# Attention scores as 256-column products of split queries and keys, and powers of lambda put in place by ScalarE

## The chip, the cores and the metric

The kernel runs on one core of one Trainium2 chip. TensorE (PE) multiplies, VectorE (DVE) and ScalarE (ACT) work element by element, GpSimd (POOL) does little here, and SyncE (SP) issues the DMAs. The metric is device time in microseconds. A change of about 0.2% is the least that a measurement of this kernel can tell from none.

## What is computed

One hybrid decoder layer over 256 tokens of 1024 features: an input projection, 32 diagonal complex state-space groups beside eight causal attention heads of 64, an output projection, a layer norm, a mixture of 16384 single-neuron experts, and a second layer norm. With one block of 256 keys the attention is plain causal attention. What matters here:

```python
lam_bar = jnp.exp(lam * dt)
b_bar = ((lam_bar - 1.0) / lam)[:, :, None] * b_c
...
s_own = jnp.einsum('bhqd,bhkd->bhqk', qf, ko) * scale
s_own = jnp.where(k_pos[None, :] <= q_pos[:, None], s_own, NEG)
p = jax.nn.softmax(jnp.concatenate([s_sel, s_own], axis=-1), axis=-1)
```

The state-space part needs the products of B and C with the powers lam_bar, lam_bar squared and so on (four time steps are taken together).

## The kernel before

The kernel is written with a scheduler that orders the instructions of each engine by the order of tracing and by what is free, and places all waits. A pool's tile with a tag has a fixed number of buffers (`bufs`); a new tile waits until the last user of the buffer's old tile is done. Instructions of one engine run in the order shown by the scheduler; an engine that waits holds up everything behind it.

The stages in order: the mixer (input projections, state space, attention, output projection, first norm), the queries and their top-16 lists on VectorE, the first matrices of the experts (`u_wide`, line 911), the gates, the second matrices (`v_mm`, line 1175) and the last norm. From the queries on the work is large fp32r products, with weights cut into a high and a low part: `split` (line 67) casts the high part on ScalarE (line 71) and subtracts on VectorE (line 72). The mixer's pieces are traced in the order of the words in `CFG['order']` (line 46), each word a branch of `do` (line 665).

Pieces that the change and the prediction touch:

- **Input projection.** `tokproj` (line 170, word u) and `chproj(1, ...)` (line 179, word q) multiply in plain fp32: one product is two passes in the trace. `chproj(2, ...)` (word k) multiplies split keys' weights with split tokens (`xsplit`, line 196: mixh and mixl), in fp32r: 96 products of 256 columns, in four quarters of 24. Both calls of `chproj` take four PSUM banks from the pool tag "w" (`pbank`, line 102, four buffers), and ScalarE copies each bank to `qk` (line 191), which is fp32.
- **State space.** `powers` (line 408) makes B or C times powers of lambda: two products per part on VectorE (lines 421 and 422), and then, since pairs of groups go to different columns of the block-diagonal Bbd or Cbd, two 64-partition operations (line 426) that add or subtract and put the result in place. `s5_min` (line 447, word min) turns Bbd on TensorE in eight groups of four transposes (line 452), and ScalarE copies each to MinT (line 454). `s5_rot` (line 466) builds rotations on VectorE in `big` buffers that `powers` uses too.
- **Masks.** `masks` (line 593, word mask, first in the order) makes `mb`, 128x128 in bf16, and `identb`.
- **Scores.** `attend(b)` (line 611) takes one block b of 128 queries, two heads at a time. A head's operands lie on 64 partitions. For each block of keys it makes a 128x128 product in fp32 (line 623) and adds the mask to the diagonal one by a product of identb and mb (line 627), on 128 partitions. For b = 0 only the first 128 keys count; for b = 1 all 256. Then VectorE takes the maximum, ScalarE the exponentials, TensorE transposes them (line 637) and ScalarE copies them to pTs. Between the heads stand the value projection's products (line 217).
- **Shared buffers.** x0 (tag "x2") holds the transposed tokens xT in its first half and the second block's transposed probabilities in the other; later x2, the normalised tokens, takes its place, and last the final weights (line 1210).

Of the kernel before, what the change touches and what calls it, by code (L numbers as in the profile page):

```python
# [8 lines left out]
F32 = mybir.dt.float32  # L9
# [32 lines left out]
def f32(ap):  # L42
    return ap.bitcast(F32)


CFG = dict(order='mask zero u par b q min rt rot xs ks k c0 c vs e0 e1 s0 v v a0 v a0 v a0 a0 v s1 a1 v a1 v a1 a1 v kin p0 o0 p1 o1 glu',
# [7 lines left out]
def layer(ctx, tc, I, out, tap=None, upto=None):  # L54
# [58 lines left out]
    with ExitStack() as px:  # L113
# [6 lines left out]
        with ExitStack() as mx:  # L120
# [9 lines left out]
            x0 = const.tile([128, 2, ND * T], F32, tag="x2", name="x0")  # L130
            xT = x0[:, 0].rearrange("p (d t) -> p d t", t=T)
# [36 lines left out]
            qk = sb.tile([128, 2, 4, T], F32, name="qk")  # L168
# [10 lines left out]
            def chproj(blk, scale, parts):  # L179
# [10 lines left out]
                for m in range(4):  # L190
                    S.activation(qk[:, blk - 1, m], pt[m], AF.Copy, scale=scale)
                return mm
# [16 lines left out]
            def vproj(pt):  # L209
                for q in range(4):  # L210
                    hi, lo = M["wv", q]
                    for k in range(2):
# [6 lines left out]
                        yield  # L219

# [187 lines left out]
            def powers(L, n, xr, xi, dst, k0, sg, EE, tmp):  # L408
# [9 lines left out]
                for i, (a, b) in enumerate(((xr, xi), (xi, xr))):  # L418
# [171 lines left out]
            mb = sb.tile([128, 128], BF, name="mb")  # L590
            identb = sb.tile([128, 128], BF, name="identb")

            def masks():
# [5 lines left out]
                for j in range(4):  # L599
                    P.iota(pq[32 * j:32 * j + 32], pattern=[[0, 1]], base=j, channel_multiplier=4,  # L600
                           allow_small_or_imprecise_dtypes=True)
                V.tensor_scalar(mb, kp.rearrange("p j c -> p (j c)"), pq, NEGBIG,
                                op0=OP.is_gt, op1=OP.mult)
                V.tensor_copy(identb, ident)
# [4 lines left out]
                   x0[:, 1].rearrange("p (n i t) -> p n i t", n=4, i=2)]  # L609

            def attend(b):
# [3 lines left out]
                for n in range(4):  # L615
# [3 lines left out]
                    pt = pbank([128, 2, T])  # L619
                    for i, h in enumerate(heads):  # L620
# [740 lines left out]
```

## Time and profile before

| what | value |
|---|---|
| median of three runs | 951.42 us (950.58 to 951.55) |
| the profiled execution's own time | 949.16 us |
| its span, first to last instruction | 947.4 us |
| mean granted TensorE clock | 0.995 of full speed |
| TensorE busy | 934.4 us (99%) |
| VectorE busy | 721.7 us (76%) |
| ScalarE busy | 562.8 us (59%) |

A profile is one execution. The busy time of an engine counts instructions from start to end; products on TensorE are pipelined and their ends are modelled, so it is the distance of their starts that tells their price. A releaser (written `<-`) is what ended an engine's idle time.

### The profile page before, as it was taken

The page shows a single profiled execution, that of the slowest core. Times are in us where ns is not written, and L with a number is a line of the kernel's source. Part 1 is how long each engine was busy: PE and PEld are TensorE (multiplying, and loading weights), DVE is VectorE, ACT ScalarE, POOL GpSimd, SP SyncE. Part 2 cuts the span into 40 slices and gives each one's busy share as a digit, 9 for nine tenths or more (in the row PEclk, how much of TensorE's full clock was granted, in tenths as well). Part 3 has the DMA queues.
Part 4 walks back from the last instruction along what each step waited for, and adds up shares of the span by engine and source line. Part 5 has one row for each costly group of instructions (what it writes and reads, how often), then busy time and mean ns, then how long its engine had stood idle before and what let it go on. Part 6 is the DMA issues. An engine that isn't in the chain of part 4 may idle for free.

```text
span 947.4 us, 15305 instructions
## 1 busy us (share of the span) xinstructions
PE 934.4 (99%) x5588; PEld 810.0 (86%) x5588; DVE 721.7 (76%) x1495; ACT 562.8 (59%) x1067; POOL 11.2 (1%) x19
## 2 busy tenths in 40 slices
PE   9999999999999999999999999999999999999996
PEld 4887889998888888999999999888888888888885
DVE  9998687998988967888898996655555555555566
ACT  4526644566575667998888776554455465445550
POOL 3000010000000000000000000000000000000000
PEclk9999999999999999999999999999999999999998
DMA  7331573356555555354444445655555585555551
GB/s 290 111 113 58 173 237 112 135 179 202 195 180 198 182 195 178 134 182 156 156 157 156 157 157 178 198 189 192 198 192 190 196 285 188 193 200 189 191 198 45
DMA packets 50075, 166.18 MB, mean 175 GB/s; under 512 B 5328, under 2 KB 9936, under 8 KB 49872
## 3 DMA queue, kind: packets, MB, share of 16 engines
q1 hardware_dynamic: 50000, 165.20, 51.3%
q8 instruction: 44, 0.72, 0.3%
q14 instruction: 31, 0.25, 0.1%
HBM read 163.09 MB, written 2.10 MB: 174 GB/s over the span
## 4 chain that ended last, share of the span: by engine, by line
PE 91%; DVE 8%; issue 1%; ACT 0%; DVEq 0%; ACTq 0%
PE pg L1180 36%; PE pw L916 16%; PE pw L1264 10%; PE pw L918 10%; PE pg L1141 3%; PE pa L1264 3%; PE pw L919 2%; PE pw L768 2%; PE psb L217 1%; PE pa L871 1%; PE pw L623 1%; PE pw L498 1%; PE psb L552 1%; PE pw L648 1%; PE pw L945 0%
## 5 line engine op out<-in xcount | busy, mean ns | idle before, releaser
L72 DVE TENSOR_TENSOR lo<-raw,hi 128x1024 fp32r<-128x1024 f32 x168 | 205.6, 1224 | 151.8 <-ACT hi L71 151.6
L71 ACT CAST hi<-raw 128x1024 fp32r<-128x1024 f32 x168 | 176.9, 1054 | 171.8 <-PE pg L1180 156.5
L1180 PE MATMUL pg<-hi,wv 128*128 128x512 f32 x988 | 264.5, 389 | 0.0
L1180 PEld LDWEIGHTS pg<-hi,wv 128*128 128x128 f32 x988 | 185.4, 188 | 38.7 <-DVE wv L1111 0.2
L916 PE MATMUL pw<-x,hi 128*128 128x512 f32 x672 | 171.2, 393 | 0.0
L1180 PE MATMUL pg<-lo,wv 128*128 128x512 f32 x494 | 152.3, 389 | 0.0
L916 PEld LDWEIGHTS pw<-x,hi 128*128 128x128 f32 x672 | 124.3, 189 | 23.2
L79 DVE TENSOR_TENSOR lo<-raw,hi 128x1024 fp32r<-128x1024 f32 x96 | 117.1, 1219 | 16.8 <-ACT hi L78 15.8
L918 PEld LDWEIGHTS pw<-x,lo 128*128 128x128 f32 x768 | 104.8, 190 | 7.4
L1180 PEld LDWEIGHTS pg<-lo,wv 128*128 128x128 f32 x494 | 92.7, 188 | 19.2
L918 PE MATMUL pw<-x,lo 128*128 128x256 f32 x768 | 107.3, 282 | 0.0
L78 ACT CAST hi<-raw 128x1024 fp32r<-128x1024 f32 x96 | 101.2, 1054 | 4.2 <-PE pa L1264 2.7
L921 ACT COPY ul<-pw 128x256 f32<-128x256 f32 x96 | 35.6, 371 | 90.1 <-PE pw L919 90.1
L1135 ACT ACTIVATE o<-eq,gL 128x128 f16<-128x128 f16 x256 | 84.3, 439 | 6.0 <-DVE eq L1131 5.4
L1264 PEld LDWEIGHTS pw<-x,hi 128*128 128x128 f32 x512 | 65.9, 189 | 1.3
L1264 PE MATMUL pw<-x,hi 128*128 128x256 f32 x512 | 66.6, 283 | 0.0
L1110 ACT CAST wv<-act 128x256 fp32r<-128x256 f32 x125 | 52.3, 419 | 0.8 <-DVE act L1147 0.8
L1111 DVE TENSOR_TENSOR wv<-act,wv 128x256 fp32r<-128x256 f32 x125 | 52.0, 417 | 0.0
L1264 PE MATMUL pw<-x,lo 128*128 128x256 f32 x256 | 38.8, 292 | 0.0
L919 PE MATMUL pw<-x,hi 128*128 128x512 f32 x96 | 38.0, 396 | 0.0
L1141 PE MATMUL pg<-o,o 128*128 128x128 f16 x512 | 36.5, 219 | 0.0
L922 DVE TENSOR_TENSOR us<-pw,ul 128x256 f32<-128x256 f32 x64 | 26.8, 418 | 11.7 <-ACT ul L921 10.9
(341 smaller groups left out, 1121.0 us busy)
## 6 DMA issues: line engine op xcount, KB each, us to landing
raw<-in_u SPq DMA_DIRECT2D x128, 512.0 KB, 3.5
raw<-in_v SPq DMA_DIRECT2D x128, 512.0 KB, 3.4
raw<-in_w_q SPq DMA_DIRECT2D x12, 512.0 KB, 4.1
raw<-in_w_in SPq DMA_DIRECT2D x8, 512.0 KB, 6.2
raw<-in_w_out SPq DMA_DIRECT2D x8, 512.0 KB, 4.1
w<-in_w_in SPq DMA_DIRECT2D x7, 512.0 KB, 8.5
raw<-in_w_q SPq DMA_DIRECT2D x8, 256.0 KB, 4.9
raw<-in_w_glu SPq DMA_DIRECT2D x2, 512.0 KB, 3.4
```

The source lines that it names most:

```text
L71: S.copy(hi, raw)
L72: eng.tensor_tensor(lo, raw, f32(hi), op=OP.subtract)
L78: S.copy(hi, raw)
L79: return hi, lo, V.tensor_tensor(lo, raw, f32(hi), op=OP.subtract)
L916: PE.matmul(pt, hi[:, 128 * d:128 * d + 128], x2[:, d], start=d == 0, stop=False)
L918: PE.matmul(pt[:, 0], lo[:, 128 * d:128 * d + 128], xh[:, d], start=False, stop=False)
L919: PE.matmul(pt, hi[:, D - 128:], x2[:, ND - 1], start=False, stop=True)
L1110: S.copy(wh, of_tile(half, i))
L1135: S.activation(o2[:, 1, i // 2, :, i % 2], eq[:, i // 2, :, i % 2], AF.Copy, scale=gL[:, t0 + i:t0 + i + 1])
L1141: PE.matmul(pt[:, i], o1[:, i // 2, :, i % 2], o2[:, k, i // 2, :, i % 2], start=k == 0, stop=k == 1)
L1180: PE.matmul(acc[b][:, c], x[:, tk], w[:, 512 * c:512 * c + 512], start=first and j == 0, stop=last and j == 2)
L1264: PE.matmul(pt, w[:, 128 * d:128 * d + 128], x[:, d], start=n == 0 and d == 0, stop=n == 2 and d == ND - 1)
```

## The change

Five edits:

1. `chproj` makes a second tile, qkl: VectorE subtracts the rounded `qk`, which is fp32r now, from the scaled bank. qkl takes the buffer of xT (tag "xA").
2. `attend` makes each head's scores as three fp32r products of 256 columns on 64 partitions (high times high, low times high, high times low), and adds the mask by a fourth on 128 partitions, for both blocks of queries alike. `mb` is now a strip of 512 columns in fp32r: zeros, the triangle, zeros, the identity. A window of 256 of its columns is the mask of a block.
3. `powers` adds or subtracts on all 128 partitions at once, in place of the first product, and ScalarE copies the two halves into Bbd or Cbd.
4. The word mask moves from the front to behind c; three of the strip's four parts are written by ScalarE.
5. x0, x2 and the final weights are each two tiles (tags "xA" and "xB") in place of one.

```diff
-CFG = dict(order='mask zero u par b q min rt rot xs ks k c0 c vs e0 ...
+CFG = dict(order='zero u par b q min rt rot xs ks k c0 c mask vs e0 ...
...
-            x0 = const.tile([128, 2, ND * T], F32, tag="x2", name="x0")
-            xT = x0[:, 0].rearrange("p (d t) -> p d t", t=T)
+            xT = const.tile([128, ND, T], F32, tag="xA", name="xT")
...
-            qk = sb.tile([128, 2, 4, T], F32, name="qk")
+            qk = sb.tile([128, 2, 4, T], F32R, name="qk")
...
                 for m in range(4):
                     S.activation(qk[:, blk - 1, m], pt[m], AF.Copy, scale=scale)
+                    V.scalar_tensor_tensor(M["qkl"][:, blk - 1, m], pt[m], scale, f32(qk[:, blk - 1, m]),
+                                           op0=OP.mult, op1=OP.subtract)
...
                     E.tensor_tensor(q, b, li, op=OP.mult)
+                    E.tensor_tensor(p, p, q, op=OP.add if i and sg > 0 else OP.subtract)
                     for g in range(2):
                         sl = slice(64 * g, 64 * g + 64)
-                        o = dst[sl, i, :, k0:k0 + n, 16 * g:16 * g + 16]
-                        E.tensor_tensor(o, p[sl], q[sl],
-                                        op=OP.add if i and sg > 0 else OP.subtract)
+                        S.copy(dst[sl, i, :, k0:k0 + n, 16 * g:16 * g + 16], p[sl])
...
-                V.tensor_scalar(mb, kp.rearrange("p j c -> p (j c)"), pq, NEGBIG,
+
+                M["mb"] = mb = sb.tile([128, 4, 128], F32R, tag="Bc", bufs=1, name="mb")
+                for n in (0, 2):
+                    S.activation(mb[:, n], ident, AF.Copy, scale=0.0)
+                S.copy(mb[:, 3], ident)
+                V.tensor_scalar(mb[:, 1], kp.rearrange("p j c -> p (j c)"), pq, NEGBIG,
                                 op0=OP.is_gt, op1=OP.mult)
-                V.tensor_copy(identb, ident)
...
-                        for kb in range(nk):
-                            o = pt[:, i, 128 * kb:128 * kb + 128]
-                            PE.matmul(o, qk[r, 0, h // 2, 128 * b:128 * b + 128],
-                                      qk[r, 1, h // 2, 128 * kb:128 * kb + 128],
-                                      start=True, stop=kb != b)
-                            if kb == b:
-                                PE.matmul(o, identb, mb, start=False, stop=True)
+                        qh, ql = (x[r, 0, h // 2, 128 * b:128 * b + 128] for x in (qk, M["qkl"]))
+                        kh, kl = (x[r, 1, h // 2] for x in (qk, M["qkl"]))
+                        for j, (x, y) in enumerate(((qh, kh), (ql, kh), (qh, kl),
+                                                    (mb[:, 384:], mb[:, 128 - 128 * b:384 - 128 * b]))):
+                            PE.matmul(pt[:, i], x, y, start=j == 0, stop=j == 3)
...
+                    M["qkl"] = const.tile([128, 2, 4, T], F32R, tag="xA", name="qkl")
                     M["q"] = chproj(1, 0.125, lambda q: [(w_in(1, q), xT)])
...
-            x2 = const.tile([128, ND, 2, T], F32R, tag="x2", name="x2")
-            xh, xl = x2[:, :, 0], x2[:, :, 1]
+            xd = [const.tile([128, 4, 2, T], F32R, tag=t, name="x2") for t in ("xA", "xB")]
+            x2 = [xd[d // 4][:, d % 4] for d in range(ND)]
+            xh, xl = ([x[:, i] for x in x2] for i in range(2))
```

How it moves instructions, at three places. Line numbers of the changed kernel are one to five higher.

First, TensorE where the key projection begins, before: pw is a bank of the pool "w", psb a bank of the transposes of Bbd, and mixh and mixl are the split tokens. A wait names the engine, not the instruction.

```order
L452 MATMUL psb<-ident,Bbd 128x128 [waits DVE_49,Activation_49]
L452 MATMUL psb<-ident,Bbd 128x128 x7
L188 MATMUL pw<-mixh,hi 128x256 [waits Activation_49,Pool_49]
L188 MATMUL pw<-mixl,hi 128x256
L452 MATMUL psb<-ident,Bbd 128x128 [waits Activation_49]
L452 MATMUL psb<-ident,Bbd 128x128 x3
L452 MATMUL psb<-ident,Bbd 128x128 [waits Activation_49]
L452 MATMUL psb<-ident,Bbd 128x128 x3
L188 MATMUL pw<-mixh,lo 128x256 [waits DVE_49]
```

And with the change:

```order
L454 MATMUL psb<-ident,Bbd 128x128 [waits DVE_49,Activation_49]
L454 MATMUL psb<-ident,Bbd 128x128 x7
L454 MATMUL psb<-ident,Bbd 128x128 [waits Activation_49]
L454 MATMUL psb<-ident,Bbd 128x128 x3
L187 MATMUL pw<-mixh,hi 128x256 [waits DVE_49,Pool_49]
L454 MATMUL psb<-ident,Bbd 128x128 [waits Activation_49]
L454 MATMUL psb<-ident,Bbd 128x128 x3
L187 MATMUL pw<-mixl,hi 128x256
L454 MATMUL psb<-ident,Bbd 128x128 [waits Activation_49]
L454 MATMUL psb<-ident,Bbd 128x128 x3
```

The first key product waited for ScalarE and stood behind two groups of transposes; now it stands behind three and waits for VectorE, and five groups stand behind it.

Second, VectorE around the first four qkl instructions, with the change (rot, big: rotations; cp: the products for Cbd):

```order
L480 TENSOR_TENSOR big_131<-rot 128x64
L476 TENSOR_TENSOR big_128<-rot 128x128 [waits DVE_49]
L481 TENSOR_TENSOR rot<-big_130,big_131 128x16x4 [waits DVE_49]
L425 TENSOR_TENSOR cp<-prm,Lam 128x1024
L191 SCALAR_TENSOR_TENSOR qkl<-pw,qk 128x256 [waits PE_49,Activation_49]
L191 SCALAR_TENSOR_TENSOR qkl<-pw,qk 128x256 [waits Activation_49] x3
L477 TENSOR_TENSOR big_129<-rot 128x128 [waits DVE_49]
```

The four that free the query's banks stand behind both products for Cbd (the first some way above) and most of the rotations up to 128 columns.

Third, TensorE where the scores of the first block begin, before (mb and identb are the mask and the identity):

```order
L516 MATMUL pa<-U,MinT 128x64 x16
L623 MATMUL pw<-qk 128x128 [waits Activation_49]
L627 LDWEIGHTS identb
L627 MATMUL pw<-mb,identb 128x128
L623 MATMUL pw<-qk 128x128 [waits Activation_49]
```

And with the change, where one head is four products:

```order
L518 MATMUL pa<-U,MinT 128x64 x16
L630 MATMUL pw<-qk 128x256 [waits DVE_49]
L630 MATMUL pw<-qk,qkl 128x256
L630 MATMUL pw<-qkl,qk 128x256
L630 MATMUL pw<-mb 128x256
L630 MATMUL pw<-qk 128x256 [waits Activation_49]
```

The products of a head are longer and one mask still ends it. The first head's products now wait for VectorE too.

## Rows read from the trace of the kernel before

**Rows 1.** The page: busy time of the engines, then the last chain by engine.

```profile
PE 934.4 (99%) x5588; PEld 810.0 (86%) x5588; DVE 721.7 (76%) x1495; ACT 562.8 (59%) x1067; POOL 11.2 (1%) x19
...
PE 91%; DVE 8%; issue 1%; ACT 0%; DVEq 0%; ACTq 0%
```

**Rows 2.** Table of stretches: length, busy per engine (PE, PEld, DVE, ACT, POOL), clock, DMA.

```profile
30.00:40.00 10.00, 10.00 (x71) 8.84 (x70) 9.97 (x32) 5.83 (x12) 0.00 (x0) 1.00 0.49 142
60.00:70.00 10.00, 10.00 (x39) 7.66 (x39) 10.00 (x18) 3.51 (x10) 0.00 (x0) 0.83 0.27 89
```

**Rows 3.** Timeline, TensorE, key projection: start us, duration us, engine, line, instruction, count, idle before.

```profile
33.92 0.36 PE L188 MATMUL pw<-mixh,hi 128*128 128x256 f32 x1
...
34.40 1.14 PE L452 MATMUL psb<-ident,Bbd 128*128 128x128 f32 x8
...
42.24 0.28 PE L188 MATMUL pw<-mixh,lo 128*128 128x256 f32 x1
42.36 0.28 PE L188 MATMUL pw<-mixh,hi 128*128 128x256 f32 x1
...
46.08 0.28 PE L188 MATMUL pw<-mixl,hi 128*128 128x256 f32 x1
46.81 0.39 PE L188 MATMUL pw<-mixh,lo 128*128 128x256 f32 x1 [0.45 <-DVE lo L72]
```

**Rows 4.** Timeline, VectorE, 10 to 46 us: powers, rotations and key weights.

```profile
10.26 0.28 DVE L602 TENSOR_SCALAR mb<-kp,pq 128x128 bf16<-128x128 f32 x1
...
24.65 0.96 DVE L421 TENSOR_TENSOR big<-Bc,LamB 128x768 f32<-128x768 f32 x1
25.52 1.91 DVE L426 TENSOR_TENSOR Bbd<-big,big 64x768 f32<-64x768 f32 x2
...
37.12 0.28 DVE L475 TENSOR_TENSOR big<-rot 128x128 f32<-128x128 f32 x1
...
38.47 0.19 DVE L414 TENSOR_SCALAR nl<-Lam 128x64 f32<-128x64 f32 x1
38.57 1.22 DVE L421 TENSOR_TENSOR cp<-prm,Lam 128x1024 f32<-128x1024 f32 x1
39.71 0.42 DVE L475 TENSOR_TENSOR big<-rot 128x256 f32<-128x256 f32 x1
...
45.53 1.22 DVE L72 TENSOR_TENSOR lo<-raw,hi 128x1024 fp32r<-128x1024 f32 x1
```

**Rows 5.** Timeline, ScalarE: the cast that waits for the key projection's first quarter.

```profile
40.28 1.05 ACT L71 CAST hi<-raw 128x1024 fp32r<-128x1024 f32 x1 [1.45 <-PE pw L188]
```

**Rows 6.** Timeline, TensorE: scores of the first block (56.73 on) and the second (69.83 on).

```profile
56.73 0.49 PE L623 MATMUL pw<-qk 64*128 64x128 f32 x2
57.15 0.23 PE L627 MATMUL pw<-mb,identb 128*128 128x128 bf16 x1
57.31 0.48 PE L623 MATMUL pw<-qk 64*128 64x128 f32 x2
...
61.54 0.78 PE L217 MATMUL psb<-hi,mixh 128*128 128x512 f32 x1
...
69.83 0.71 PE L623 MATMUL pw<-qk 64*128 64x128 f32 x4
70.47 0.23 PE L627 MATMUL pw<-mb,identb 128*128 128x128 bf16 x1
70.63 0.71 PE L623 MATMUL pw<-qk 64*128 64x128 f32 x4
71.27 0.23 PE L627 MATMUL pw<-mb,identb 128*128 128x128 bf16 x1
71.31 0.48 PE L217 MATMUL psb<-wv,mixh 128*128 128x512 f32 x1
```

**Rows 7.** Timeline, TensorE's weight loads: the mask's identity and a head's keys or queries.

```profile
57.15 0.10 PEld L627 LDWEIGHTS <-identb 128*128 128x128 bf16 x1
57.31 0.18 PEld L623 LDWEIGHTS pw<-qk 64*128 64x128 f32 x1
```

More of the change, by code (lines that the diff above doesn't have):

```diff
@@ L43, in f32 @@
     return ap.bitcast(F32)
-CFG = dict(order='mask zero u par b q min rt rot xs ks k c0 c vs e0 e1 s0 v v a0 v a0 v a0 a0 v s1 a1 v a1 v a1 a1 v kin p0 o0 p1 o1 glu',
+CFG = dict(order='zero u par b q min rt rot xs ks k c0 c mask vs e0 e1 s0 v v a0 v a0 v a0 a0 v s1 a1 v a1 v a1 a1 v kin p0 o0 p1 o1 glu',
            glu='VV',
@@ L219, in vproj @@
                         yield
+            M = {}
             pw = sb.tile([128, 44, NPAIR], F32, name="pw")
@@ L601, in masks @@
                            allow_small_or_imprecise_dtypes=True)
-                V.tensor_scalar(mb, kp.rearrange("p j c -> p (j c)"), pq, NEGBIG,
+                M["mb"] = mb = sb.tile([128, 4, 128], F32R, tag="Bc", bufs=1, name="mb")
[3 more added lines that the diff above has]
+                V.tensor_scalar(mb[:, 1], kp.rearrange("p j c -> p (j c)"), pq, NEGBIG,
                                 op0=OP.is_gt, op1=OP.mult)
-                V.tensor_copy(identb, ident)
             rs = sb.tile([128, 2, 8], F32, name="rs")
             pTs = [sb.tile([128, 4, 2, 128], F32, name="pT0"),
-                   x0[:, 1].rearrange("p (n i t) -> p n i t", n=4, i=2)]
+                   const.tile([128, 4, 2, 128 * 2], F32, tag="xB", name="pT1")]
             def attend(b):
@@ L619, in attend @@
                     pt = pbank([128, 2, T])
+                    mb = M["mb"].rearrange("p n t -> p (n t)")
                     for i, h in enumerate(heads):
[L621 to L627 removed]
+                        qh, ql = (x[r, 0, h // 2, 128 * b:128 * b + 128] for x in (qk, M["qkl"]))
[3 more added lines that the diff above has]
+                            PE.matmul(pt[:, i], x, y, start=j == 0, stop=j == 3)
                     mx_ = sb.tile([128, 2], F32, tag="mx", bufs=2, name="mx_")
@@ L829, in ln_apply @@
                         PE.transpose(pt[:, i], h1[:, 128 * k:128 * k + 128], ident)
-                    st["xh", b] = S.copy(xh[:, 4 * c:4 * c + 4, 128 * b:128 * b + 128], pt)
+                    st["xh", b] = S.copy(xd[c][:, :, 0, 128 * b:128 * b + 128], pt)
                 nc.sync.dma_start(res_d[b], h1)
@@ L836, in ln_low @@
                 for c in range(2):
-                    o = slice(4 * c, 4 * c + 4), slice(128 * b, 128 * b + 128)
-                    st["low"] = V.tensor_sub(xl[:, o[0], o[1]], st[b, c], f32(xh[:, o[0], o[1]]))
+                    tk = slice(128 * b, 128 * b + 128)
+                    st["low"] = V.tensor_sub(xd[c][:, :, 1, tk], st[b, c], f32(xd[c][:, :, 0, tk]))
             W4 = []
@@ L870, in query4 @@
                     for d in range(8):
-                        PE.matmul(pt, x[:, d, tk], W4[d // 2][y][:, 512 * (d % 2):512 * (d % 2) + 512],
+                        PE.matmul(pt, x[d][:, tk], W4[d // 2][y][:, 512 * (d % 2):512 * (d % 2) + 512],
                                   start=j == 0 and d == 0, stop=j == 2 and d == 7)
@@ L915, in u_wide @@
         for d in range(ND - 1):
-            PE.matmul(pt, hi[:, 128 * d:128 * d + 128], x2[:, d], start=d == 0, stop=False)
+            PE.matmul(pt, hi[:, 128 * d:128 * d + 128], x2[d], start=d == 0, stop=False)
         for d in range(ND):
-            PE.matmul(pt[:, 0], lo[:, 128 * d:128 * d + 128], xh[:, d], start=False, stop=False)
-        PE.matmul(pt, hi[:, D - 128:], x2[:, ND - 1], start=False, stop=True)
+            PE.matmul(pt[:, 0], lo[:, 128 * d:128 * d + 128], xh[d], start=False, stop=False)
+        PE.matmul(pt, hi[:, D - 128:], x2[ND - 1], start=False, stop=True)
         ul = pool.tile([128, T], F32, tag="ul", bufs=bufs, name="ul")
@@ L1209, in layer @@
     v_mm(1, t, False, True, (1,))
-    xs = const.tile([128, 2, 2, 1024], F32R, tag="x2", name="vx")
+    xs = [const.tile([128, 2, 1024], F32R, tag=t, name="vx") for t in ("xA", "xB")]
     last, st = [], {}
@@ L1214, in layer @@
         if 3 <= i < 5:
-            own = xs[:, 0, i - 3], xs[:, 1, i - 3]
+            own = xs[i - 3][:, 0], xs[i - 3][:, 1]
             w = gk.tile([128, 2, T], F32R, tag="ga", bufs=2, name="wx")
@@ L1263, in dense @@
         for d in range(ND):
-            PE.matmul(pt, w[:, 128 * d:128 * d + 128], x[:, d], start=n == 0 and d == 0,
+            PE.matmul(pt, w[:, 128 * d:128 * d + 128], x[d], start=n == 0 and d == 0,
                       stop=n == 2 and d == ND - 1)
```

3 lines of the change are left out of this document (removed).

## Prediction

> **What bounds the kernel now.** I read the page first: TensorE is busy for 99% of the span and carries 91% of the chain that ended last [rows 1]. A busy TensorE need not be one at full use, so I went to the stretch that the change touches. In the table of stretches TensorE is full from 30 to 40 us and from 60 to 70 us, but VectorE is full too (9.97 and 10.00 of 10), and in the second one the granted clock averages 0.83 where the first has 1.00 [rows 2]. Two full engines raise the question which one the other waits for. TensorE's timeline answers it: in the key projection the 256-column products start 0.12 us apart, and between 34 and 50 us TensorE stands still for one wait that it shows, 46.81, released by VectorE's low half of the last key weights. From 46.08 to 46.81 one product takes 0.73 us, so that wait costs 0.61 us [rows 3]. So VectorE works all the time, and TensorE hardly ever waits for it. A microsecond taken from VectorE is then worth nothing by itself; one added to TensorE, or one for which TensorE stands still, comes out at the end, because what follows the attention (output projection, experts) is TensorE's chain again.
>
> **VectorE's copies that go to ScalarE.** Each of the two Bbd parts was two 64-partition subtractions, 1.91 us for the pair; now it is one of 128x768 at 0.87 us (the start of one L421 to the next instruction) [rows 4], and ScalarE makes two copies. VectorE saves 1.04 us twice. For Cbd a pair (1.91 x 4/3 = 2.5 us, by the columns) becomes one 128x1024 operation of 1.14 us (38.57 to 39.71) [rows 4], which saves about 1.4 us twice. Together some 4.9 us less, against eight new qkl instructions: the nearest row is a 128x256 operation of 0.42 us; the next one starts some 0.09 us before an instruction's end (24.65 + 0.96 against 25.52) [rows 4], so 0.33 us in a row and 2.7 us in all. VectorE ends about 2 us lighter. ScalarE has 5.8 busy us of 10 in 30 to 40 [rows 2] and takes its copies in gaps. I cost both at nothing, since TensorE is what ends this stage.
>
> **The new wait: four PSUM banks.** The pool "w" has four banks. The query projection fills all four, and the key projection needs the same four. Before, ScalarE's copies alone freed them, and the first key product started at 33.92 [rows 3]. Now VectorE must read each bank as well, and its queue holds the four qkl instructions behind a long line of other work. When does it get there? VectorE was never idle here, so its time can be counted from a row: before, at 38.47 (nl), it had done all that now stands ahead of qkl [rows 4], with four differences. The mask's two instructions are gone from the front: minus 0.3 (0.28 for the one that moves, the other is alike) [rows 4]. The two Bbd parts: minus 2.1. Rot instructions from 37.12 to 38.47 now come later: minus 1.35. The scaling nl and both products for cp now come earlier: plus 0.1 and twice 1.14. So qkl begins near 37.0 and its first bank is free at 37.4. Until then TensorE can do one more group of Bbd transposes than before (34.40, two groups in some 0.9 us) [rows 3] and then stands still from about 34.9 to 37.4: 2.5 us. Everything else of the key projection is queued behind it on TensorE, five of the eight transpose groups among it, and behind those ScalarE's copies of them to MinT.
>
> Before, the first quarter took from 33.92 [rows 3] to 40.28, when ScalarE's cast got its buffer from it [rows 5]: 6.36 us with six groups inside. Now five are inside, 0.4 us less: 37.4 + 5.9 = 43.3, some 3.0 us late. The 0.61 us wait at 46.81 goes, since VectorE reaches that low half in time: it began it at 45.53 [rows 4], and 45.53 - 0.3 - 2.1 + 4 x 0.33 + 2 x 1.14 = 46.7, done by 47.9, while TensorE asks for it after two more quarters of 24 x 0.12 us, at 49.1. So the key projection ends **2.4 us later** (bounds 1.6, if ScalarE's pace on the transposes is made up, and 3.0, if nothing of the wait is won back).
>
> **The scores on TensorE.** Now: first block of queries, eight heads, 56.73 to the first value product at 61.54, 4.81 us; second block 0.80 us a head (69.83 to 70.63), less about 0.3 where other work follows, 6.1 us [rows 6]. Together 10.9 us. One head of the first block has two 128-column passes and one mask: 56.73 to 57.15 and 57.15 to 57.31. One of the second has four passes: 69.83 to 70.47 [rows 6]. The difference is two passes in 0.22 us, 0.11 each; what remains of 0.42 is 0.21 us that a head pays beside its columns when TensorE goes to the 64-row operands and leaves them. The mask streams 128 bf16 columns, about half of a 0.11 us pass, and takes 0.16 us, so 0.11 of it is again going there and back. It isn't the number format: from the bf16 mask at 71.27 to the fp32r value product at 71.31, both with 128 rows, only 0.04 us pass [rows 6]. The changed kernel still goes from 64 rows to 128 and back in every head. Its columns: four products of 256, at 0.12 us each by the key projection's fp32r rows [rows 3]. So a head costs 3 x 0.12 + 0.21 + 0.12 + 0.11 = 0.80 us; sixteen cost 12.8, less 0.3 where other work follows: 12.5 us, **1.6 us more** than now. The second block breaks even, the first loses 0.22 us a head, because its masked half is now computed too. Lower bound: no cost for going there and back, 16 x 4 x 0.12 = 7.7 us, 3.2 less than now. Upper bound: the mask's weights, a bf16 identity before and fp32r now, load in 0.18 us rather than 0.10, as the fp32 weights beside them do [rows 7], and show the 0.08 us in every head: 2.9 more than now. I take 0.80, since [rows 6] are the very place.
>
> The Trainium skill, "TensorE: Matmul & The Clock Gate", section "Part 3: Packing small matmuls — row/col tiling", says that a weight load overlaps running matmuls only where the row group differs. By that the three 64-row products of a head would each show their load. This trace disagrees: four passes on the same 64 rows, each with weights of its own, run 0.11 us apart [rows 6]. Were it so for these products, the sum would be some 3.4 us higher, the 32 loads that rival 4 counts.
>
> **The clock.** Before, 60 to 70 us lost (1 - 0.83) x 10 = 1.7 us to a granted clock of 1.2 GHz for part of it, right behind the first block's scores [rows 2]. The rows ahead of it are the sparsest of the stage (0.27 us of streaming in 0.58 us). Now it is 0.43 us in 0.80, of 64 rows for the most part, and longer. I let the fall stay: 0, with bounds of -1.7 (it goes) and +1.7 (a second one, for the new standstill).
>
> **Edits at nothing.** xT, x2 and the last weights in two tiles keep their readers' order; the mask moves behind c, where VectorE reaches it some 9 us before the first score. If VectorE were late there, scores would wait, but it gains 2 us.
>
> **Sum.** 2.4 + 1.6 + 0 = 4.0 us. Against the profiled execution's own 949.16 us (947.4 of span) that is 953.2. This execution lies 2.3 below the median of 951.42, to which the forecast refers: **955.4 us**. A measurement here can tell about 0.2%, 1.9 us, from no change. Bounds on the forecast's own terms: 953.4 (stall 1.6, a head at 0.73 us) to 958.8 (3.0 + 2.9 and most of a second clock fall).
>
> **Rivals.**
> 1. *Denser scores.* The cost beside the columns belongs to the old fp32 passes and bf16 mask. A head then takes 0.48 us, scores 3.2 us less, and such dense products keep the clock: -1.7. With the stall +2.4: **948.9 us**, faster. For it: no row here has fp32r operands of 64 rows, so the cost beside the columns is carried over from fp32. Against: 71.27 to 71.31 and the jumps at 64 rows [rows 6]. Below 0.55 us a head without the clock, or 0.66 with it, it outweighs the stall. Chance 0.20.
> 2. *The clock fall goes, the rest as forecast:* **953.7 us**. For it: a larger share of streaming. Chance 0.12, half of it inside 0.2%.
> 3. *Both prices half:* TensorE wins back half of the stall in later gaps and a head costs 0.70 us: 1.2 + 0 us, **952.6 us**, no change that shows. Chance 0.12. Here the change does move work from VectorE to ScalarE, as it does in all the cases, without doing anything for the time.
> 4. *No overlap of loads at 64 rows:* two loads a head, 32 in all, each as long as one 0.11 us pass of 128 columns [rows 6], come on top: 3.4 us, **958.8 us**. For it: longer moving operands are new here. Against: the 0.11 us themselves. Chance 0.06.
>
> The forecast has 0.50. Faster: 0.20. Within 0.2%: 0.12 + 0.06 = 0.18. Slower: 0.50 + 0.06 + 0.06 = 0.62. The range goes from rival 1 to rival 4, 948.8 to 958.8; what is beyond (rival 1 with a smaller stall, a second clock fall on top) I put at 0.2. The likeliest case alone: 953.4 to 958.8.
>
> **What would show it.** Right: on TensorE, no product between about 35 and 37.4 us, and the first key product released by VectorE's qkl; the wait for the low half near 47 gone; a head's scores 0.75 to 0.85 us from start to start; everything from the value projection on later by about 4 us at like durations. Wrong: key products that start before 35 us, heads of about 0.5 us, or a granted clock of 1.00 from 55 to 75 us; and if the output projection started no later than now, TensorE was not what ended this stage.

## The result, and the profile after

The changed kernel takes 956.3 us (median of four runs, 954.66 to 957.29) where the kernel before, beside it on the same chip, takes 951.0: ratio 1.0058, 95% interval 1.0046 to 1.0071. A second measurement on another occasion (e11 below) gives 955.73 us against 950.34, ratio 1.0055 (1.0041 to 1.0069). The forecast was 955.4. Slower, then, by 5.3 to 5.4 us.

Two executions of the changed kernel were profiled. The first takes 957.29 us (span 955.5), the highest of its runs; the one of e11 955.72 (span 953.9), next to its median. They agree within 0.01 us up to the scores. What sets them apart is the clock, which falls in both and stays down longer in the first.

The page of the first one, busy time and the chain, against [rows 1]:

```profile
PE 940.7 (98%) x5588; PEld 813.8 (85%) x5588; DVE 718.9 (75%) x1498; ACT 570.9 (60%) x1078; POOL 11.2 (1%) x19
...
PE 91%; DVE 7%; issue 1%; ACT 0%; DVEq 0%; ACTq 0%
```

VectorE has 2.8 us less work, ScalarE 8 us more, and the chain is TensorE's as before. The table of stretches, against [rows 2]:

```profile
30.00:40.00 10.00, 8.60 (x56) 7.27 (x54) 10.00 (x30) 6.18 (x15) 0.00 (x0) 1.00 0.63 207
60.00:70.00 10.00, 10.00 (x30) 7.17 (x31) 4.47 (x8) 0.00 (x0) 0.00 (x0) 0.59 0.05 20
```

TensorE is no longer full from 30 to 40 us, and from 60 to 70 its clock averages 0.59 (before 0.83) while VectorE runs out of work. TensorE's timeline shows both places, against [rows 3] and [rows 6]:

```profile
33.63 1.04 PE L454 MATMUL psb<-ident,Bbd 128*128 128x128 f32 x8
34.91 0.66 PE L454 MATMUL psb<-ident,Bbd 128*128 128x128 f32 x4 [0.24 <-ACT MinT L456]
36.73 0.36 PE L187 MATMUL pw<-mixh,hi 128*128 128x256 f32 x1 [1.16 <-DVE qkl L191]
...
58.12 0.38 PE L630 MATMUL pw<-qk 64*128 64x256 f32 x1
58.35 0.28 PE L630 MATMUL pw<-qk,qkl 64*128 64x256 f32 x1
58.47 0.27 PE L630 MATMUL pw<-qkl,qk 64*128 64x256 f32 x1
58.67 0.38 PE L630 MATMUL pw<-mb 128*128 128x256 f32 x1
58.98 0.38 PE L630 MATMUL pw<-qk 64*128 64x256 f32 x1
...
62.84 0.58 PE L630 MATMUL pw<-qk 64*128 64x256 f32 x1
...
64.29 0.58 PE L630 MATMUL pw<-qk 64*128 64x256 f32 x1
...
66.46 0.79 PE L218 MATMUL psb<-hi,mixh 128*128 128x512 f32 x1
```

The first key product waits for VectorE's qkl, which frees the bank. A head goes from 58.12 to 58.98: 0.86 us. Its starts lie 0.23, 0.12, 0.20 and 0.31 us apart, so what is beyond four times 0.12 stands where it comes to the 64 rows, where it leaves them for the mask, and behind the mask. At 1.2 GHz, the lower level of the clock, one goes from 62.84 to 64.29: 1.45 us. And VectorE, against [rows 4]:

```profile
35.04 1.22 DVE L425 TENSOR_TENSOR cp<-prm,Lam 128x1024 f32<-128x1024 f32 x1
36.17 1.41 DVE L191 SCALAR_TENSOR_TENSOR qkl<-pw,qk 128x256 fp32r<-128x256 f32 x4
...
45.80 1.22 DVE L72 TENSOR_TENSOR lo<-raw,hi 128x1024 fp32r<-128x1024 f32 x1
```

Where the time went is read from five marks on TensorE, start times in us, one line for each profiled execution. L518 (L516 before) is the first product with MinT, behind the key projection; "scores" and "values" are the first products of the scores and of the value projection; "gate" is the first product of the word glu.

| kernel | first key product | L518 | scores | values | gate | span |
|---|---|---|---|---|---|---|
| before | 33.92 | 49.55 | 56.73 | 61.54 | 108.71 | 947.4 |
| changed | 36.73 | 50.94 | 58.12 | 66.46 | 115.77 | 955.5 |
| changed, again (e11) | 36.74 | 50.95 | 58.13 | 65.54 | 114.40 | 953.9 |
| e1 copies alone | 34.17 | 49.67 | 59.63* | 56.73* | 108.03 | 947.5 |
| e2 VectorE writes | 36.73 | 52.76 | 59.94 | 68.64 | 118.12 | 957.5 |
| e3 powers behind | 36.48 | 52.55 | 59.73 | 68.23 | 117.85 | 957.4 |
| e5 rotation behind too | 34.28 | 49.17 | 56.35 | 65.32 | 114.18 | 953.5 |
| e4 no mask | 36.74 | 52.22 | 59.40 | 61.37 | 106.65 | 945.4 |
| e6 padded keys | 36.87 | 51.57 | 58.63 | 62.54 | 121.67 | 958.8 |
| e12 bf16 mask | 36.74 | 52.14 | 59.32 | 65.39 | 112.73 | 951.4 |
| e7 pairs of halves | 36.73 | 50.93 | 57.99 | 61.00 | 104.87 | 944.4 |
| e8 pairs, rotation behind | 33.65 | 48.54 | 55.60 | 59.82 | 109.03 | 948.6 |
| e9 before, pairs | 34.65 | 49.69 | 56.78 | 61.23 | 106.67 | 945.2 |
| e10 before, pairs, copies | 34.63 | 49.83 | 59.71* | 56.89* | 102.52 | 942.1 |

(* twelve value products go ahead of the scores there.) From the gate to the end every row but e6 needs 838.5 to 839.8 us (e6 837.2), so nearly all that matters lies ahead of it. In e11 the gate comes 5.7 us later than before (114.40 against 108.71), and these come from three places: 1.4 up to L518; 16 heads, 8 x (0.86 - 0.58) + 8 x (0.86 - 0.80) = 2.7; and the clock, which is at 0.66 from 60 to 70 us and so loses 3.4 us instead of 1.7. Together 5.8.

### The profile page after: what moved, and what is told of

Its sections match the earlier page's. It is cut to its first block, busy times and chain, and to the rows that moved or that the text cites. A ratio compares the mean times of both kernels' runs of the same rounds, so it can differ in the third digit from the quotient of the medians.

```text
span 955.5 us, 15318 instructions
## 1 busy us (share of the span) xinstructions
PE 940.7 (98%) x5588; PEld 813.8 (85%) x5588; DVE 718.9 (75%) x1498; ACT 570.9 (60%) x1078; POOL 11.2 (1%) x19
## 4 chain that ended last, share of the span: by engine, by line
PE 91%; DVE 7%; issue 1%; ACT 0%; DVEq 0%; ACTq 0%
PE pg L1185 35%; PE pw L921 16%; PE pw L1269 10%; PE pw L923 10%; PE pg L1146 3%; PE pa L1269 2%; PE pw L924 2%; PE pw L772 2%; PE pw L630 2%; PE psb L218 1%; PE pw L187 1%; PE pa L876 1%; PE pw L500 1%; PE psb L554 1%; PE pw L651 1%
```

## The experiments

**VectorE's part.** My theory was that TensorE ends the stage and is held up only by what stands ahead of qkl on VectorE. e1 makes the powers edit alone in the kernel before:

```diff
+                    E.tensor_tensor(p, p, q, op=OP.add if i and sg > 0 else OP.subtract)
                     for g in range(2):
                         sl = slice(64 * g, 64 * g + 64)
-                        o = dst[sl, i, :, k0:k0 + n, 16 * g:16 * g + 16]
-                        E.tensor_tensor(o, p[sl], q[sl],
-                                        op=OP.add if i and sg > 0 else OP.subtract)
+                        S.copy(dst[sl, i, :, k0:k0 + n, 16 * g:16 * g + 16], p[sl])
```

> The kernel before with only the powers edit: VectorE forms a part's result in place and ScalarE's copies put it into Bbd and Cbd. Theory (TensorE ends this stage, VectorE hardly keeps it waiting): VectorE loses some 4.5 us of work, the only wait it can shorten is the 0.61 us one for the last key low half, so 950.4 to 951.2 against 951.0. Rival (a full VectorE sets the pace of the stage): 2 us or more gained, 949 or less. Second rival (ScalarE's eight copies delay the Bbd transposes and its casts): 1 us or more lost.

Measured: 949.37 us, ratio 0.9991 (0.9982 to 1.0000), a gain of 0 to 1.7 us. The wait of [rows 3] for the low half shrinks from 0.45 to 0.31 us, but L518 comes no earlier (49.67 against 49.55): up to there the work taken from VectorE is worth nothing, as the first theory has it. The 0.7 us that the gate gains come from behind it. Twelve value products now go ahead of the scores and more go between the heads, and the clock, which cost 1.7 us before, stays at 1.00 from 55 to 75 us; what takes about 1 us of that back isn't shown. e2 is the changed kernel with that diff turned round:

> The changed kernel with the powers edit undone: VectorE writes Bbd and Cbd by halves again. Theory (the key projection waits for VectorE's low halves of the queries, and these stand behind VectorE's other work): VectorE reaches them some 2 us later than the 36.2 us of the changed kernel, the first key product starts near 38.7 instead of 36.7, and the whole is 1 to 2 us longer, 957.3 to 958.3 against 956.3. Rival (the standstill is made by something else, or hidden later): within 0.5 us of the changed kernel.

Measured: 959.34 us, ratio 1.0090 (1.0075 to 1.0105), 3 us above the changed kernel. The loss is there, not by the way I gave: qkl begins at 36.17 us, the first key product at 36.73, to the hundredth where they were. What grew is the idle time ahead of it, 2.35 us in place of 1.16 (Bbd is done later, so only two groups of transposes are there to fill it), and at its end the clock falls: 0.83 from 30 to 40 us, which costs 1.7. L518 is 1.8 us later.

So qkl stays at 36.2 us with more work on VectorE too. e3 puts the powers for Cbd behind the last qkl of the queries (`low` in the loop of `chproj`):

```diff
...
+                if blk == 1:
+                    M["ql"] = low
...
                 elif w == "c":
-                    s5_c()
+                    with tc.issue_after(M["ql"].ins):
+                        s5_c()
```

> The changed kernel with the powers of lambda for Cbd issued behind the low halves of the queries, so that on VectorE nothing of cp stands ahead of qkl. Theory (the standstill at 35.5 to 36.7 is VectorE's queue): the first key product starts by 35.2 us, the 1.2 us wait goes, the key projection ends about 1.2 us earlier, 955.1 against 956.3. The scores and the clock stay: a head 0.86 us. Rival (what VectorE now does later is waited for in its turn: cp for the kernel Kin, the low half near 46 us): no gain, 956.3.

Measured: 957.51 us, ratio 1.0071 (1.0056 to 1.0087): not better. The first key product starts at 36.48, behind 2.38 us of standstill, and the clock falls there too (0.67 from 35 to 40 us). VectorE's timeline of e3:

```profile
34.93 0.41 DVE L478 TENSOR_TENSOR big<-rot 128x256 f32<-128x256 f32 x1
35.26 0.28 DVE L483 TENSOR_TENSOR rot<-big,big 128x128 f32<-128x128 f32 x1
35.58 0.42 DVE L479 TENSOR_TENSOR big<-rot 128x256 f32<-128x256 f32 x1
35.92 1.41 DVE L191 SCALAR_TENSOR_TENSOR qkl<-pw,qk 128x256 fp32r<-128x256 f32 x4
```

The rotation took the place of the powers. By e2 and e3 the scheduler fills VectorE's row with whatever it has until the point where it plans qkl; taking one piece away brings another forward. e5 therefore moves the rotation behind qkl as well:

```diff
                 elif w == "rot":
-                    s5_rot()
+                    with tc.issue_after(M["ql"].ins):
+                        s5_rot()
```

> The changed kernel with both the rotation tables (rot) and the powers of lambda for Cbd issued behind the low halves of the queries: the run before this one moved only the powers, and the rotation's operations took their place ahead of qkl, which began at 35.9 us as before (36.2). Theory (what decides is what stands ahead of qkl on VectorE, whatever it is): qkl begins by 33.5 us, the first key product by 34.5, the standstill goes, L518 begins some 1.5 us earlier than in the changed kernel (50.9), 954.3 to 955.3 against 956.3. The heads stay at 0.86 us. Rival (TensorE waits for the next late thing on VectorE, the fourth low half of the key weights or the rotation in the scan): no gain, 956 or more.

Measured: 955.71 us, ratio 1.0059 (1.0046 to 1.0073), the changed kernel's own. The standstill is gone, the first key product starts at 34.28 and L518 1.8 us earlier, as the theory has it; but the gate comes only 0.2 us earlier than in e11. What took the gain isn't the rival's wait (VectorE holds TensorE up nowhere there), it is the clock. Stretches of e5, and of e11:

```profile
60.00:65.00 5.00, 5.00 (x16) 3.44 (x15) 5.00 (x8) 0.29 (x2) 0.00 (x0) 0.50 0.41 147
65.00:70.00 5.00, 5.00 (x13) 3.97 (x13) 5.00 (x11) 1.32 (x8) 0.00 (x0) 0.50 0.01 3
```

```profile
60.00:65.00 5.00, 5.00 (x21) 3.42 (x22) 4.48 (x8) 0.00 (x0) 0.00 (x0) 0.81 0.11 43
65.00:70.00 5.00, 5.00 (x13) 3.81 (x14) 0.00 (x0) 0.00 (x0) 0.00 (x0) 0.50 0.01 3
```

e5 loses 5.0 us there, e11 3.4. Why the fall is longer in e5 stays open; its mean clock is 0.990 to 0.992 over its runs, that of e11 0.991 to 0.993.

**The heads.** e4 leaves the mask product out:

```diff
-                        for j, (x, y) in enumerate(((qh, kh), (ql, kh), (qh, kl),
-                                                    (mb[:, 384:], mb[:, 128 - 128 * b:384 - 128 * b]))):
-                            PE.matmul(pt[:, i], x, y, start=j == 0, stop=j == 3)
+                        for j, (x, y) in enumerate(((qh, kh), (ql, kh), (qh, kl))):
+                            PE.matmul(pt[:, i], x, y, start=j == 0, stop=j == 2)
```

> The changed kernel without the mask product (the scores aren't masked; all else stays). A head is then three 256-column products of 64 rows and nothing else. Theory (a head pays for its columns and, apart from them, for going from 64 rows to 128 for the mask and back): without the mask nothing changes rows from head to head, a head falls from 0.86 us to 0.36 to 0.42 us, so 16 heads give some 7 us, and with the denser products the long fall of the clock (10.2 us at half speed) shortens, up to 3 us more: 946 to 949.5. Rival (the products of 64 rows are slow by themselves): only the mask's own 0.12 us a head goes, 1.9 us in all, 954.4, heads of 0.74 us and the same fall of the clock.

Measured: 946.90 us, ratio 0.9960 (0.9946 to 0.9973), some 9 us below the changed kernel, in spite of a fall of the clock at its standstill (0.83 from 30 to 40 us). The theory's size, and more than its reason. Its first block on TensorE:

```profile
59.40 0.38 PE L629 MATMUL pw<-qk 64*128 64x256 f32 x1
59.63 0.28 PE L629 MATMUL pw<-qk,qkl 64*128 64x256 f32 x1
59.74 0.27 PE L629 MATMUL pw<-qkl,qk 64*128 64x256 f32 x1
59.75 0.38 PE L629 MATMUL pw<-qk 64*128 64x256 f32 x2
59.97 0.28 PE L629 MATMUL pw<-qk,qkl 64*128 64x256 f32 x2
60.09 0.28 PE L629 MATMUL pw<-qkl,qk 64*128 64x256 f32 x2
...
61.37 0.50 PE L218 MATMUL psb<-hi,mixh 128*128 128x512 f32 x1
```

Eight heads take 1.97 us, 0.25 each: from 59.97 on two products of a kind start together, 0.12 us a pair. By the kernel's text they belong to a head on rows 0 to 63 and one on rows 64 to 127; e7 puts that to the test. So two things had changed at once, and e6 takes one alone: keys padded with zeros to 128 rows, so that nothing changes rows and nothing runs side by side.

```diff
...
+                    for g, sl in enumerate(halves2):
+                        S.activation(kp_[sl, g, m], pt[m][sl], AF.Copy, scale=scale)
+                        V.scalar_tensor_tensor(M["kl"][sl, g, m], pt[m][sl], scale, f32(kp_[sl, g, m]),
+                                               op0=OP.mult, op1=OP.subtract)
...
+                        qh, ql = (x[:, h // 2, 128 * b:128 * b + 128] for x in (qh_, ql_))
-                        kh, kl = (x[r, 1, h // 2] for x in (qk, M["qkl"]))
+                        kh, kl = (x[:, h % 2, h // 2] for x in (kp_, M["kl"]))
```

> The changed kernel with each head's keys padded with zeros to 128 rows (the other head's half is zero), so that all four products of a head use 128 rows and TensorE never goes from 64 rows to 128 within the scores; the columns stay the same. Theory (a head pays for going to 64 rows and back, by rows of before 0.21 us and 0.11 us): a head falls from 0.86 us to 0.48 us, 16 heads give 6 us, and with the denser products the long fall of the clock shortens or goes, up to 3 us more: 947 to 950.5. Rival (what went away with the mask product in the run without it was something else, such as two heads running side by side on the two halves of the rows): heads stay above 0.7 us, 954 or more.

Measured: 960.58 us, ratio 1.0117 (1.0101 to 1.0132). The whole tells nothing of the heads: to make room I had put pTs of the second block into MinT's tile, whose place the scan's states need, and the states then waited for the value products (VectorE stands idle 1.96 us for them at 95.67, TensorE 1.72 us at 99.42, and from 100 to 120 us the clock is at 0.50). The heads, long before that, are what was asked for:

```profile
59.66 0.40 PE L642 MATMUL pw<-kp__120,qx 128*128 128x256 f32 x2
59.90 0.28 PE L642 MATMUL pw<-kl,qx 128*128 128x256 f32 x1
60.02 0.28 PE L642 MATMUL pw<-mb 128*128 128x256 f32 x1
60.14 0.40 PE L642 MATMUL pw<-kp__120,qx 128*128 128x256 f32 x2
...
62.54 0.40 PE L231 MATMUL psb<-hi,mixh 128*128 128x512 f32 x1
```

0.48 us a head with the same columns and the same mask, and the clock is 1.00 from 60 to 70 us. The 0.38 us between that and 0.86 are the way to 64 rows and back. Part of them is the load of the mask's weights, says e12, which makes the mask's strip, identity and all, bfloat16:

```diff
-                M["mb"] = mb = sb.tile([128, 4, 128], F32R, tag="Bc", bufs=1, name="mb")
+                M["mb"] = mb = sb.tile([128, 4, 128], BF, tag="Bc", bufs=1, name="mb")
```

> The changed kernel with the mask and its identity in bfloat16 (all else, the 256 columns too, stays). Theory (a head pays for the load of the mask's weights, which no running product covers when TensorE comes from 64 rows: 0.19 us with the fp32r identity, 0.10 with a bfloat16 one): from the mask to the next head 0.22 instead of 0.31 us, a head 0.77 to 0.78 instead of 0.86, 16 heads give 1.3 us, 1.0041 of the time before against 1.0055 to 1.0058; a little more if the fall of the clock gets shorter. Rival (the 0.31 us are the going back to 64 rows alone): the head stays at 0.86 us and the time at 1.0055.

Measured: from a mask to the next head 0.21 us, a head 0.77 (60.07 to 60.84), as the theory has it. The load of the mask's weights in the changed kernel, then in e12, and a head of e12:

```profile
58.66 0.19 PEld L630 LDWEIGHTS pw<-mb 128*128 128x128 f32 x1
...
59.86 0.10 PEld L630 LDWEIGHTS <-mb 128*128 128x128 bf16 x1
...
60.07 0.38 PE L630 MATMUL pw<-qk 64*128 64x256 f32 x1
...
60.63 0.28 PE L630 MATMUL pw<-mb 128*128 128x256 bf16 x1
60.84 0.38 PE L630 MATMUL pw<-qk 64*128 64x256 f32 x1
```

The edit also makes the mask's 256 columns bfloat16. That is worth next to nothing: in e9 below two bfloat16 products of 256 columns start 0.11 to 0.12 us apart, as fp32r ones do (0.12). The time, 954.13 us and 1.0049 (1.0035 to 1.0062), moves the right way but by less than these intervals can tell. In the profiled execution a fall of the clock at the standstill, which the changed kernel doesn't have (0.74 from 35 to 40 us, 0.92 from 40 to 45), costs 1.7 us, and the fall in the scores is shorter (0.69 from 65 to 70).

**The order of the heads.** e7 uses what e4 showed. For every four heads the mask comes first, one 512-column product for each of two banks, then the products alternate between the halves of the rows:

```diff
...
+                        for pt in pts:
+                            PE.matmul(pt, mb[:, 3], mb[:, None, 1 - b:3 - b].to_broadcast([128, 2, 2, 128]),
+                                      start=True, stop=False)
+                        for i in range(2):
+                            c = n + i
+                            for j, (x, y) in enumerate(((0, 0), (1, 0), (0, 1))):
+                                for g in range(2):
+                                    r = slice(64 * g, 64 * g + 64)
+                                    q_, k_ = ((qk, M["qkl"])[z] for z in (x, y))
+                                    PE.matmul(pts[g][:, i], q_[r, 0, c, 128 * b:128 * b + 128], k_[r, 1, c],
+                                              start=False, stop=i == 1 and j == 2)
```

> The changed kernel with the scores in another order: for every four heads first the mask, one 512-column product for each of two banks, then the twelve 64-row products, alternating between a head on rows 0 to 63 and one on rows 64 to 127. Theory (in the run without the mask, 18 of 24 products of the first block began two at a time, 0.12 us a pair, because they lie on different halves of the rows): four heads take 2 x 0.23 us for the mask, 6 x 0.12 for the pairs and 0.3 for going to 64 rows and back, 1.4 to 1.5 us, 0.36 a head against 0.86; 16 heads give 8 us; with the long fall of the clock shortened, up to 3 us more: 945 to 948.5. Rival (no two products run at once where a 128-row product is near): four heads 2.2 us, 16 heads give 5 us at most, 950.5 to 952.

Measured: 946.17 us, ratio 0.9960 (0.9947 to 0.9974), 9 us below the changed kernel and 4 below the one before.

```profile
57.99 0.71 PE L624 MATMUL pw<-mb 128*128 128x512 f32 x2
58.63 0.39 PE L632 MATMUL pw<-qk 64*128 64x256 f32 x2
58.86 0.28 PE L632 MATMUL pw<-qk,qkl 64*128 64x256 f32 x2
58.98 0.28 PE L632 MATMUL pw<-qkl,qk 64*128 64x256 f32 x2
...
59.54 0.73 PE L624 MATMUL pw<-mb 128*128 128x512 f32 x2
```

Four heads in 1.55 us, 0.39 each, and the clock stays at 1.00 from 60 to 70 us; 3.4 of the 9.5 us by which its gate comes ahead of e11's are the clock's. The standstill for qkl is still in it (2.01 us idle). e8 takes e3's and e5's edits to it:

```diff
-                    s5_c()
+                    with tc.issue_after(M["ql"].ins):
+                        s5_c()
...
-                    s5_rot()
+                    with tc.issue_after(M["ql"].ins):
+                        s5_rot()
```

> The two edits before together: rotation and powers behind the low halves of the queries, and the scores with the mask first and the heads alternating between the halves of the rows. Theory (standstill and scores lie one behind the other on TensorE, so that their gains add): the time of the alternating heads alone less 1 to 2 us, 943 to 947.5. Rival (one gain hides the other): the same as the alternating heads alone.

Measured: 950.42 us, ratio 0.9999 (0.9990 to 1.0009): neither, it loses 4 us. L518 comes 2.4 us earlier than in e7, and TensorE waits the gain away for the scan, which is now late on VectorE (L531 reads the banks that the value products need), with a fall of the clock behind it (0.51 from 70 to 75 us):

```profile
59.82 0.47 PE L220 MATMUL psb<-hi,mixh 128*128 128x512 f32 x1 [1.04 <-DVE big L531]
...
69.89 0.54 PE L647 MATMUL pa<-ident,p 128*128 128x128 f32 x2 [1.96 <-DVE big L531]
```

If the order is what pays, the split of queries and keys has no part in it. e9 orders the heads of the kernel before in that way, float32 products and bfloat16 mask as they were:

```diff
...
+                        for pt in pts:
+                            PE.matmul(pt[:, :, :w], identb, mb[:, None, 1 - b:2].to_broadcast([128, 2, nk, 128]),
+                                      start=True, stop=False)
+                        for i in range(2):
+                            for g in range(2):
+                                r = slice(64 * g, 64 * g + 64)
+                                PE.matmul(pts[g][:, i, :w], qk[r, 0, n + i, 128 * b:128 * b + 128],
+                                          qk[r, 1, n + i, :w], start=False, stop=i == 1)
```

> The kernel before, unsplit float32 queries and keys and all, with only the order of its scores changed as in the run that beat it: for every four heads first the mask, now one product for each of two banks, then the heads alternating between rows 0 to 63 and rows 64 to 127. Theory (what a head pays is the going to 64 rows and back, and two products on different halves of the rows run at once; the split into halves has no part in it): the first block takes some 2.2 us (before 4.8), the second 2.5 (6.1), the clock doesn't fall, and there is no standstill for the low halves: 942 to 945 against 950.2 to 951. Rival (the gain of the alternating heads needs the 256-column products of split operands, since a float32 product is made of several passes): less than 4 us gained, 947 or more.

Measured: 947.51 us, ratio 0.9969 (0.9957 to 0.9981). Its first block:

```profile
56.78 0.38 PE L621 MATMUL pw<-mb,identb 128*128 128x256 bf16 x2
57.09 0.71 PE L626 MATMUL pw<-qk 64*128 64x128 f32 x8
57.74 0.39 PE L621 MATMUL pw<-mb,identb 128*128 128x256 bf16 x2
58.06 0.71 PE L626 MATMUL pw<-qk 64*128 64x128 f32 x8
61.23 0.47 PE L217 MATMUL psb<-hi,mixh 128*128 128x512 f32 x1 [2.46 <-DVE big L527]
```

Float32 products pair up too: four heads in 0.96 us (before 2.31). But then TensorE stands still for 2.46 us. The theory's scores were right and its total was not, because VectorE, full from 30 to 70 us, ends the stage as soon as TensorE is that much faster: the first value product starts at 61.23, only 0.3 us earlier than before. The clock falls behind the standstill too (0.83 from 60 to 70 us). e10 adds e1's edit:

```diff
+                    E.tensor_tensor(p, p, q, op=OP.add if i and sg > 0 else OP.subtract)
...
+                        S.copy(dst[sl, i, :, k0:k0 + n, 16 * g:16 * g + 16], p[sl])
```

> The run before this one with the change's powers edit added (ScalarE's copies put the powers of lambda in place). Theory (VectorE's relief is worth up to 1 us, as it was alone: 0.9991 of the time before): 0 to 1 us below the alternating heads alone. Rival (with shorter scores VectorE, which was full from 30 to 70 us, ends the stage, so that its relief now counts): 2 us or more below.

Measured: 943.86 us, ratio 0.9928 (0.9914 to 0.9941), 3.7 us below e9: the rival. The 2.46 us wait is gone, and with it the fall of the clock (1.00 from 60 to 70 us), which cost e9 1.7 us; behind the gate e10 needs 1.0 us more. What ScalarE took over stood ahead of the scan on VectorE, here in e9:

```profile
54.45 2.45 DVE L426 TENSOR_TENSOR Cbd<-cp 64x1024 f32<-64x1024 f32 x2
...
60.40 0.68 DVE L527 TENSOR_TENSOR big<-psb,rot 128x512 f32<-128x512 f32 x1
```

and in e10 the scan's last reads of that bank are done by 54.83:

```profile
53.55 0.69 DVE L524 TENSOR_TENSOR big<-psb,rot 128x512 f32<-128x512 f32 x1 [0.16 <-PE psb L515]
54.15 0.68 DVE L526 TENSOR_TENSOR big<-psb,rot 128x512 f32<-128x512 f32 x1
```

This is the fastest version of the study. It keeps one edit of the change, the copies, and leaves the split out. Last, e11 is the changed kernel with no edit:

> The changed kernel as it is, once more, so that the runs that undo a part of it have a reference of as many runs as their own. Theory: 1.0058 of the time before, within 0.001, a fall of the clock of some 7 to 10 us that begins in the first block of scores. If its median lies 1 us or more above that of the run with rotation and powers behind the low halves (1.0059), the standstill was worth that much; if not, the gain is given back behind it.

Measured: 955.73 us, 1.0055 (1.0041 to 1.0069), and a shorter fall of the clock than in the first profile. Its median equals that of e5, so the second half of its expectation holds: the gain of e5 is given back.

## Why the prediction was right, point by point

- **What bounds the stage.** TensorE, as said: the copies alone change almost nothing (e1). But "a microsecond taken from VectorE is then worth nothing by itself" holds only up to the next limit. That limit was near: in e9 VectorE releases the first value product at 61.23, against 61.54 before, and past that point the same edit gives 3.7 us (e10), part of it by the clock.
- **The new wait.** The mechanism is as predicted: four banks, qkl behind a long row on VectorE, three groups of transposes first, the first key product released by qkl, and no wait for the low half near 47 us. The size was 2.4 us and came out at 1.4: qkl begins at 36.17, not 37.0. I counted which of VectorE's instructions would stand ahead of it; e2 and e3 show that the scheduler fills that row up to much the same point in any case.
- **A head.** 0.80 us was forecast, 0.86 came. The step that went wrong is the choice between two ends: I set aside the load of the mask's fp32r weights, the upper bound, and e12 shows it in every head (0.77 with bfloat16 weights). From the mask to the next head I had 0.23 us, and it is 0.31. 16 x 0.06 = 1.0 us. (The 10.9 us that the forecast takes off for the old scores hold some 0.2 us of the clock's fall, 60.77 to 61.54 for the eighth head, which it counts with the clock too.) The rest of the step, that going from 64 rows to 128 and back costs what the columns don't explain, is shown by e6: 0.48 us with 128 rows throughout, which is the 4 x 0.12 of my lower bound.
- **The clock.** "I let the fall stay: 0." It got longer: 1.7 us more in e11, 3.4 in the first profile (0.59 from 60 to 70 us, 0.80 from 70 to 75), the second beyond my bound of 1.7. The bound was for a second fall at the new standstill; in both profiles it is the one fall in the scores that got longer, while e2, e3, e4 and e12 do have one at the standstill. This is the term that was mis-sized most. (The 0.43 us of streaming that it gives a head are 4 x 0.12 = 0.48 by its own rows.)
- **The sum.** 1.4 + 2.7 + 1.7 = 5.8 us in e11 against 2.4 + 1.6 + 0 = 4.0. Errors of -1.0, +1.1 and +1.7 partly cancel, so the forecast came nearer to the median (955.4 against 955.7 and 956.3) than its terms deserved. A part of that is luck of the base as well: I added to 951.42, and the kernel before measured 951.0 and 950.3 beside the changed one. As a difference, 4.0 us were forecast and 5.3 to 5.4 came.
- **The rivals.** Denser scores: no head near 0.48 us. But its second half was sound: where heads do take 0.48 us or less and no standstill follows (e4, e6, e7, e10), the clock stays at 1.00 behind them. The clock fall that goes, and both prices half: no. No overlap of loads: no, the third product on the same 64 rows starts 0.12 us behind the second (58.35, 58.47), with the fp32r operands for which no row stood before; the 0.23 us from the first to the second come only with the way to the 64 rows (in e4's second block two heads follow one another on 64 rows, 68.44 to 69.14, and from the third of their six products on each starts 0.12 us behind the last).

## What to carry to other kernels

In this kernel products on 64 partitions are cheap only in company: put those on the lower and the upper half next to each other, so that two run at once, and gather what needs all 128 rows (here the mask, as the first product of a bank) into few places. A second reader of a PSUM bank on a busy engine is a wait of the next stage, and with this scheduler the row ahead of that reader fills up again unless everything that could go there is held back (e3, e5). Before calling relief of a full engine worthless, ask by how much it is not the bound: after the other engine got faster, the same copies were worth 3.7 us, some of it by a clock that no longer fell.

## What had not been expected of the hardware

Two products on different halves of the rows run side by side, 0.12 us a pair of 256 columns (e4, e7), and float32 ones as well (e9). The Trainium skill, "TensorE: Matmul & The Clock Gate", "Part 3: Packing small matmuls — row/col tiling", says that matmuls on different row groups run at once; the rows agree. It also says that matmuls start strictly in program order. In e4 the kernel's text has head after head, three products each, with two heads in a row on the same half; yet the first products of two heads start at 59.75 and 59.86, ahead of the second product of either (59.97). If the scheduler kept the order of the text, it isn't kept across the halves on TensorE; no row shows the program's order, so this stays open.

The clock fell to 1.2 GHz while TensorE was busy all the time, in the course of eight heads in a row of 0.58 us or more each (before, changed, e2, e3, e5, e11, e12). In e1 such heads stand in groups of two and four with value products between, and the clock stays at 1.00; from 55 to 75 us it also stays in e4, e6, e7 and e10, whose heads take less. In e8 and e9 they take less too, but there are standstills of 1.04 and 1.96 us (e8) and 2.46 us (e9), and the clock falls (0.51 from 70 to 75 us, and 0.83 from 60 to 70). With a standstill ahead of the key projection came a fall in some profiles (1.40 us in e12, 1.85 in e4, 2.35 in e2, 2.38 in e3) and none in others (1.16 in the changed kernel, 2.01 in e7, 2.38 in e6). What decides in either place isn't shown.
